# Split GELU multiply: outputs packed into the first load's buffer, 64 KB stores in place of separate output buffers

## Chip, cores, metric

One core of a Trainium2 chip. The metric is device time in microseconds; the granted clock was 1.00 in every run. Times are medians, with the range of the runs in brackets. A run over 1.5% above the fastest of its kernel counts as slow and is left out.

## The reference

```python
x: float32 [32, 512, 2048]
x1, x2 = x[..., :1024], x[..., 1024:]
return 0.5 * x1 * (1 + erf(x1 / sqrt(2))) * x2     # float32 [32, 512, 1024]
```

134.2 MB are read and 67.1 MB written. Per output element there is one GELU (ScalarE, "ACT" in the profile) and one multiply (VectorE, "DVE").

## The kernel before

The 16384 rows are cut into 16 tiles of 8 rows on each of 128 partitions. Loads go out from SyncE ("SP", queue q1), stores from ScalarE (queue q10). Two load buffers of 64 KB a partition and two output buffers of 32 KB take 192 KB.

```python
R, STEP = 8, 4
x_t = x_flat.rearrange("(n p r) d -> n p r d", p=P, r=R)
o_t = out_flat.rearrange("(n p r) d -> n p r d", p=P, r=R)
xpool = ctx.enter_context(tc.tile_pool(name="xpool", bufs=2))
opool = ctx.enter_context(tc.tile_pool(name="opool", bufs=2))
# ... cut: load(i) is one nc.sync.dma_start of a whole tile
ahead = [load(0), load(1)]
for i in range(n_tiles):
    x_tile = ahead.pop(0)
    o_tile = opool.tile([P, R, half], out.dtype, name="o_tile")
    for r in range(0, R, STEP):
        rows = slice(r, r + STEP)
        nc.scalar.activation(out=x_tile[:, rows, :half], in_=x_tile[:, rows, :half], func=GELU)
        nc.vector.tensor_mul(out=o_tile[:, rows, :], in0=x_tile[:, rows, :half], in1=x_tile[:, rows, half:])
        # ... cut: the last tile is stored in two halves
    # ... cut: the last two tiles are stored from nc.sync
    store(nc.scalar, i, o_tile, slice(0, R))
    if i + 2 < n_tiles:
        ahead.append(load(i + 2))
```

## Time and profile before

| | before |
|---|---|
| time | 471.43 us (471.22 to 471.63, 5 runs) |
| span of the profiled run | 469.7 us |
| ACT busy / DVE busy | 115.2 us / 140.2 us |
| DMA rate over the span / in mid-kernel | 429 / 434 GB/s |
| one tile: load in flight, store in flight | 45.5 us, 41.8 us (medians from issue to landing) |

Read it from the bottom up: a load and a store are in flight all the time, the rate does not move (434 GB/s in every stretch of 58 us from 57 to 405 us), and the compute engines wait for it (ACT 340.5 us for loads, DVE 321.6 us for ACT). (Issue is the moment at which an instruction starts a transfer, landing the moment at which its completion is signalled.)

### The profile page before, as it was taken

Reading aid. Unit: us, or ns where it says so; the run is one execution under the profiler, and the core shown is the slowest. Engines: PE = TensorE matmul, PEld = TensorE weight load, DVE = VectorE, ACT = ScalarE, POOL = GpSimd, SP = SyncE. Lnnn points to the kernel's source line nnn. Section 1 sums busy time; section 2 is a strip of 40 time slices with the busy share of each in tenths; the row PEclk is TensorE's granted clock in tenths of the full one; section 3 lists DMA queues with packets and bytes.
Section 4 is the critical chain, followed back from the end, with each engine's and each line's share of the span. In section 5 each row is a group of like instructions: output and inputs, shape, how many; then the busy total and the mean of one; then the engine's idle time right before and its main releaser. Section 6 shows DMA issues by size and latency. Waiting matters only on the chain.

```text
span 469.7 us, 213 instructions
## 1 busy us (share of the span) xinstructions
DVE 140.2 (30%) x32; ACT 115.2 (25%) x33; POOL 0.2 (0%) x4
## 2 busy tenths in 40 slices
DVE  0070704307042070520606115060250702507043
ACT  1052306023060320603206041060500505005060
POOL 0000000000000000000000000000000000000000
DMA  8999999999999999999999999999999999999988
GB/s 357 446 446 357 446 446 446 402 446 458 391 446 444 433 463 402 435 413 491 402 419 430 491 402 402 446 491 402 402 446 480 413 402 444 449 446 402 474 375 357
DMA packets 4754, 201.35 MB, mean 429 GB/s; under 512 B 528, under 2 KB 528, under 8 KB 528
## 3 DMA queue, kind: packets, MB, share of 16 engines
q1 hardware_dynamic: 2736, 142.61, 70.5%
q10 hardware_dynamic: 2016, 58.72, 29.0%
q14 instruction: 2, 0.02, 0.0%
HBM read 134.22 MB, written 67.11 MB: 429 GB/s over the span
## 4 chain that ended last, share of the span: by engine, by line
DMA 77%; DVE 14%; ACT 6%; DVEq 1%; issue 0%; SPq 0%; ACTq 0%
DMA x_tile<-in_x_dram 77%; DVE o_tile L57 14%; ACT x_tile L54 6%; DVEq L93 1%; SPq L41 0%; ACTq L54 0%
## 5 line engine op out<-in xcount | busy, mean ns | idle before, releaser
L57 DVE TENSOR_TENSOR o_tile<-x_tile 128x4096 f32<-128x4096 f32 x32 | 140.2, 4422 | 321.6 <-ACT x_tile L54 321.6
L54 ACT ACTIVATE x_tile<-x_tile 128x4096 f32<-128x4096 f32 x32 | 114.0, 3608 | 340.5 <-DMA x_tile<-in_x_dram 340.5
L54 ACT ACT_TABLE_LOAD x1 | 1.3, 1283 | 0.7 <-PEq L82 0.7
L82 POOL MEMSET const-bfloat16-1.0<- 128x1 bf16 x1 | 0.1, 102 | 0.0
L82 POOL MEMSET const-uint8-127<- 128x1 uint8 x1 | 0.1, 101 | 0.0
L82 POOL MEMSET const-float32-0.0<- 128x1 f32 x1 | 0.1, 99 | 0.2 <-issue 0.2
L82 POOL MEMSET const-float32-1.0<- 128x1 f32 x1 | 0.1, 98 | 0.0
## 6 DMA issues: line engine op xcount, KB each, us to landing
out_dram<-o_tile ACTq DMA_DIRECT2D x14, 4096.0 KB, 41.8
out_dram<-o_tile SPq DMA_DIRECT2D x1, 4096.0 KB, 24.8
out_dram<-o_tile SPq DMA_DIRECT2D x2, 2048.0 KB, 6.9
x_tile<-in_x_dram SPq DMA_DIRECT2D x16, 45.5
```

What stands on the lines that cost most here:

```text
L54: nc.scalar.activation(out=x_tile[:, rows, :half], in_=x_tile[:, rows, :half], func=GELU)
L57: nc.vector.tensor_mul(out=o_tile[:, rows, :], in0=x_tile[:, rows, :half], in1=x_tile[:, rows, half:],)
L82: nc = _bacc.Bacc("TRN2", target_bir_lowering=False, num_devices=1)
L93: with _tile.TileContext(nc) as tc:
```

## The change

Intent: a third full load buffer instead of output buffers, and stores as long as loads. A block is now 16 rows a partition, read as two loads A and B of 8 rows each. A has two buffers, B one. A's outputs overwrite A's first half, row by row behind the reading; B's outputs go into A's second half. The whole A buffer, 64 KB a partition, is then one store. The diff is shortened: "..." and the comments mark cuts, and the helpers `load`, `gelu` and `gelu_mul` are left out.

```diff
-    R, STEP = 8, 4
-    x_t = x_flat.rearrange("(n p r) d -> n p r d", p=P, r=R)
-    o_t = out_flat.rearrange("(n p r) d -> n p r d", p=P, r=R)
+    R = 8
+    x_t = x_flat.rearrange("(n p h r) d -> n h p r d", p=P, h=2, r=R)
+    o_t = out_flat.rearrange("(n p r) d -> n p r d", p=P, r=2 * R)
...
-    xpool = ctx.enter_context(tc.tile_pool(name="xpool", bufs=2))
-    opool = ctx.enter_context(tc.tile_pool(name="opool", bufs=2))
+    apool = ctx.enter_context(tc.tile_pool(name="apool", bufs=2))
+    bpool = ctx.enter_context(tc.tile_pool(name="bpool", bufs=1))
...
+    ahead = [load(0), load(1), load(2)]
+    for n in range(n_blocks):
+        a_tile, b_tile = ahead.pop(0), ahead.pop(0)
+        last = n == n_blocks - 1
+        gelu(a_tile, slice(0, 4))
+        gelu(a_tile, slice(4, R))
+        for lo, hi in ((0, 1), (1, 2), (2, 4), (4, 8)):
+            gelu_mul(slice(lo, hi), a_tile, a_tile[:, lo * half : hi * half])
...                                # last block: store A's half from nc.sync
+        for lo, hi in ((0, 4), (4, 8)):
+            gelu(b_tile, slice(lo, hi))
+            o = a_tile[:, (R + lo) * half : (R + hi) * half]
+            gelu_mul(slice(lo, hi), b_tile, o)
...                                # last block: store each quarter from nc.sync
+        if not last:
+            nc.scalar.dma_start(out=o_t[n], in_=a_tile.rearrange("p (r d) -> p r d", d=half))
+        for k in (2 * n + 3, 2 * n + 4):      # B of the next block, A of the one after
+            if k < 2 * n_blocks:
+                ahead.append(load(k))
```

Two waits are new. The next B load waits for the multiplies on the only B buffer. The A load after next waits for the landing of the whole store, since the store reads the buffer that this load fills; below it is called the **A reload**.

More of the change, by code (lines that the diff above doesn't have):

```diff
@@ L29 @@
     half = dim // 2
-    R, STEP = 8, 4
-    x_t = x_flat.rearrange("(n p r) d -> n p r d", p=P, r=R)
-    o_t = out_flat.rearrange("(n p r) d -> n p r d", p=P, r=R)
-    n_tiles = x_t.shape[0]
-    xpool = ctx.enter_context(tc.tile_pool(name="xpool", bufs=2))
-    opool = ctx.enter_context(tc.tile_pool(name="opool", bufs=2))
-    def load(i):
-        x_tile = xpool.tile([P, R, dim], x.dtype, name="x_tile")
-        nc.sync.dma_start(out=x_tile, in_=x_t[i])
-        return x_tile
-    def store(queue, i, o_tile, rows):
-        queue.dma_start(out=o_t[i][:, rows, :], in_=o_tile[:, rows, :])
@@ L47 @@
-    ahead = [load(0), load(1)]
-    for i in range(n_tiles):
-        x_tile = ahead.pop(0)
-        o_tile = opool.tile([P, R, half], out.dtype, name="o_tile")
-        last = i == n_tiles - 1
-        for r in range(0, R, STEP):
-            rows = slice(r, r + STEP)
-            nc.scalar.activation(
-                out=x_tile[:, rows, :half], in_=x_tile[:, rows, :half], func=GELU
-            )
-            nc.vector.tensor_mul(
-                out=o_tile[:, rows, :],
-                in0=x_tile[:, rows, :half],
-                in1=x_tile[:, rows, half:],
-            )
-            if last:
-                store(nc.sync, i, o_tile, rows)
-        if not last:
-            store(nc.sync if i == n_tiles - 2 else nc.scalar, i, o_tile, slice(0, R))
-        if i + 2 < n_tiles:
-            ahead.append(load(i + 2))
+    R = 8
@@ new lines, with load @@
+    x_t = x_flat.rearrange("(n p h r) d -> n h p r d", p=P, h=2, r=R)
+    o_t = out_flat.rearrange("(n p r) d -> n p r d", p=P, r=2 * R)
+    n_blocks = x_t.shape[0]
+    apool = ctx.enter_context(tc.tile_pool(name="apool", bufs=2))
+    bpool = ctx.enter_context(tc.tile_pool(name="bpool", bufs=1))
+    def load(n):
+        n, h = divmod(n, 2)
+        pool, name = (bpool, "b_tile") if h else (apool, "a_tile")
+        t = pool.tile([P, R * dim], x.dtype, name=name)
+        nc.sync.dma_start(out=t.rearrange("p (r d) -> p r d", d=dim), in_=x_t[n, h])
+        return t
@@ new lines, in gelu_mul, with gelu @@
+    def gelu_mul(rows, t, o):
+        i = t.rearrange("p (r d) -> p r d", d=dim)[:, rows, :]
+        nc.vector.tensor_mul(
+            out=o.rearrange("p (r d) -> p r d", d=half), in0=i[:, :, :half], in1=i[:, :, half:]
+        )
+    def gelu(t, rows):
+        i = t.rearrange("p (r d) -> p r d", d=dim)[:, rows, :half]
+        nc.scalar.activation(out=i, in_=i, func=GELU)
+    ahead = [load(0), load(1), load(2)]
[6 more added lines that the diff above has]
+            gelu_mul(slice(lo, hi), a_tile, a_tile[:, lo * half : hi * half])
+        if last:
+            nc.sync.dma_start(
+                out=o_t[n][:, :R, :],
+                in_=a_tile[:, : R * half].rearrange("p (r d) -> p r d", d=half),
+            )
+        for lo, hi in ((0, 4), (4, 8)):
+            gelu(b_tile, slice(lo, hi))
+            o = a_tile[:, (R + lo) * half : (R + hi) * half]
+            gelu_mul(slice(lo, hi), b_tile, o)
+            if last:
+                nc.sync.dma_start(
+                    out=o_t[n][:, R + lo : R + hi, :],
+                    in_=o.rearrange("p (r d) -> p r d", d=half),
+                )
+        if not last:
+            nc.scalar.dma_start(
+                out=o_t[n], in_=a_tile.rearrange("p (r d) -> p r d", d=half)
+            )
+        for k in (2 * n + 3, 2 * n + 4):
+            if k < 2 * n_blocks:
+                ahead.append(load(k))
```

## The prediction

Passages whose figures no trace of this case shows are cut from the text on record: one whole paragraph; in step 3 the times of the multiplies, which came to a sum of 144 us of DVE time, and the line that expects this sum; in the rivals the size of a loss by pitch and the arguments for and against it, and a limit of the rate; in step 4 a reason for the first store's wait. The sum of the forecast, its terms: 471.4 us, plus 0 or 6.5, plus 0 to 6, so 471.4 to 483.9, put at 473.5 within 470.0 to 479.5. The DVE time is not one of them.

> **What bounds the kernel now.** I read the page of the kernel before first, because its busy shares and its DMA slices say at once whether a compute engine or the transfers set the time.
>
> ```profile
> span 469.7 us, 213 instructions
> ...
> DVE 140.2 (30%) x32; ACT 115.2 (25%) x33; POOL 0.2 (0%) x4
> ...
> DMA  8999999999999999999999999999999999999988
> ...
> q1 hardware_dynamic: 2736, 142.61, 70.5%
> q10 hardware_dynamic: 2016, 58.72, 29.0%
> ...
> HBM read 134.22 MB, written 67.11 MB: 429 GB/s over the span
> DMA 77%; DVE 14%; ACT 6%; DVEq 1%; issue 0%; SPq 0%; ACTq 0%
> ```
>
> The compute engines are idle more than two thirds of the time. The DMA digit is 9 in every slice but the first and the last two, and the packets of the two queues took 70.5 + 29.0 = 99.5% of what 16 engines have in the span. The chain's "DVE 14%, ACT 6%" must not be read as 20% to be won: the chain follows a load back to the multiply that freed its buffer, but the DMA engines went on with other transfers during that multiply. The view by stretches of time settles it; its last two columns are DMA share and GB/s, the second from the left is the length:
>
> ```profile
> 57.00:115.00 58.00, 17.52 (x4) 14.25 (x4) 0.00 (x0) 1.00 1.00 434
> 173.00:231.00 58.00, 17.52 (x4) 14.24 (x4) 0.00 (x0) 1.00 1.00 434
> 440.00:470.00 30.00, 8.76 (x2) 7.12 (x2) 0.00 (x0) 1.00 0.90 385
> ```
>
> Two tiles in 58.0 us, again and again, with the DMA share at 1.00 and 434 GB/s. Two tiles are 16.78 MB in and 8.39 MB out, 25.17 MB / 434 GB/s = 58.0 us. So nothing but bytes is in the middle of the kernel, and all of 134.22 + 67.11 = 201.33 MB at 434 GB/s is 463.9 us. The other 5.8 us of the span are at the ends. From the timeline and the single packet records of the trace: the first load is issued at 0.73 us and its first packet moves at 1.7; the first packet of each engine takes 0.7 us longer than the 2.42 us of all later 64 KB packets; when the very first store joins the loads, at about 42 us, the load packet ahead of it takes 3.1 to 3.8 us instead of 2.42, 1.1 us more on the mean of the 16 engines; and the last bytes move at 468.2, 1.5 us before the end. That is 5.0 us; the rest is small gaps and the rounding of 434.
>
> Last, how the two queues share the engines, from the DMA view of the stretch 50 to 60 us (packets, MB, share):
>
> ```profile
> q1 hardware_dynamic: 48, 3.15, 72.5%
> q10 hardware_dynamic: 48, 1.57, 36.4%
> ```
>
> Equal counts of packets, twice the bytes: q1, all loads here, moves 64 KB a packet (8 rows of 8 KB), q10, all stores, 32 KB (8 rows of 4 KB). Loads and stores alternate packet by packet. That is why a 4 MB store that needs 9.7 us alone takes a median 41.8 us from issue to landing: at a third of the rate it needs 29.0 us, and it queues behind the store before it.
>
> [...]
>
> **The change, part by part.**
>
> 1. Bytes: none saved. A block of 16 rows a partition still reads 16.78 MB and writes 8.39 MB. Loads keep 64 KB packets, now from rows 128 KB apart; stores go from 32 KB to 64 KB packets, so 14 of them become 7. The gain of fewer packets is nil, as 32 KB packets already move at the full rate (1.00 share, 434 GB/s with both kinds).
>
> 2. SBUF: 2 x 64 + 2 x 32 = 192 KB a partition before, 2 x 64 + 64 = 192 KB after. The third full load buffer replaces the output buffers.
>
> 3. ACT: the same 32 GELUs, 115 us. DVE: per block 2 multiplies of 1024, one of 2048 and 3 of 4096 in place of 4 of 4096. [...] All of it lies beside transfers.
>
> 4. Waits. Before, each load needs only its own buffer's multiplies. Now the first load of a block (A) may be issued only when the whole store of two blocks ago has landed, because its buffer holds the outputs; the second (B) needs the multiplies on the single B buffer. Whether a queue runs dry is a matter of a cycle that I follow by hand, with 8.39 MB / 434 = 19.3 us for 8 MB alone, and 12.4 us from the landing of B to its last multiply (before: 22.67 to 35.11 us). A0 lands at 22.7, B0 at 42.0, A1's last byte would move at 60.5. B0 is computed at 54.5: store 0 and load B1 are issued. The first store of before was issued at 35.1 and moved its first packet at 42.3[...]. So store 0 and B1 both start at about 60.5, right as A1 ends. Now both have 64 KB packets, share half and half, and need 38.7 us: both end at about 97 to 99. If the store has the first turn it ends one packet (2.4 us) before B1 on each engine. Load A2 is issued at the landing (about 0.4 us after the last record) and can move 1.0 us later (from 457.45 to 458.3 us in the tail of before a new transfer took 0.9 us). So A2 arrives just as B1's last packet finishes. B1 lands at 100, A2 runs alone for the 12.4 us of B1's computing, has 6 us left when store 1 and B2 are issued at 112.5, and the cycle repeats, 58.0 us later. The margin is only about 1 us, but it corrects itself: if A2 is late by a little, the next store is ahead of it by as much.
>
> 5. The join. Before, stores are always two deep after the first, so a store joins a load-only stream once. After, the store queue empties in each block, so a store joins afresh 7 times. If each join costs the 1.1 us seen once, that is 6 x 1.1 = 6.5 us more. If that was a first-use cost, nothing.
>
> 6. Ends. Start: unchanged. Tail: A7's half store (4 MB) is queued behind B7 on the same queue, then two stores of 2 MB (4.8 us each) behind it: B7's last byte at about 448, then 457.7, 462.5, 467.3; the multiplies are ready at 452, 456.5 and 461, ahead of their turns. The same end as before, within 0.5 us.
>
> Sum: 471.4 us (the span plus 1.7), plus 0 or 6.5 us for the joins, plus 0 to 6 us for late A loads.
>
> **The rivals.** First, the new wait on the store bites: if B goes ahead of the store, A2 is issued about 1.4 us after the last packet of both, up to 2 us idle in each of 6 reloads, up to 12 us or 2.5%, to about 483. For it: the nearly equal ends in step 4. Against it: the self-correction, which lets it happen once or in part. Second, the 128 KB pitch costs rate[...]. Third, a gain: the chain shows DVE and ACT on 20% of the path, which a third load buffer seems to take out. That would be worth 90 us if it were real; the 1.00 DMA share speaks against it[...].
>
> **Range and chances.** About half of the weight lies on 470.5 to 472 (bytes only), a third on 475 to 479 (joins or late loads in each block), the rest above. Between these I put 473.5, with 470.0 to 479.5 as the range. 2% below, 462.0, is less than the bytes need at 434 GB/s, so faster has 1%. 2% above is 480.9, which needs two of the losses together: 9%.
>
> **What would show it.** The DMA share should stay near 1.00 with a repeat of 58.0 us a block; 59 us with dips at the joins would show step 5; a share under 0.98 just before each A load, with the load's issue waiting for the store, the first rival; a rate below 434 in stretches with share 1.00, the second. Stores should land about 43 us after issue, and in a stretch where both queues run they should now have equal bytes. [...] I am wrong if the span is below 467 or above 479.

## The result

484.27 us (483.16 to 485.49, 5 runs), slower: ratio 1.0267, 95% interval 1.0248 to 1.0286. A ratio here is the mean time of one kernel's fast runs over that of the other's of the same rounds, so not quite the ratio of the medians. The range of the prediction ended at 479.5. The changed kernel also scatters by 2.3 us, where the kernel before scatters by 0.4.

The page of the changed kernel, the lines that answer to those shown of before:

```profile
span 481.1 us, 204 instructions
...
DVE 143.4 (30%) x48; ACT 115.2 (24%) x33; POOL 0.2 (0%) x4
...
DMA  8999999999999999999999999999999999999988
...
q1 hardware_dynamic: 2736, 142.61, 70.7%
q10 hardware_dynamic: 1008, 58.72, 28.2%
...
HBM read 134.22 MB, written 67.11 MB: 419 GB/s over the span
...
DMA b_tile<-in_x_dram 58%; DMA out_dram<-a_tile 18%; DVE a_tile L50 10%; DMA a_tile<-in_x_dram 6%; ACT b_tile L56 5%; DVEq L114 1%; SPq L44 0%; ACTq L56 0%
```

The digits of the DMA row are the same 9s as before, and still 11 us are gone: a tenth is too coarse, and a packet that takes longer than most still counts as busy (below, a share of 0.99 at 417 GB/s). The rate over the span says it (419 instead of 429 GB/s), and the chain has a new member: a store, 18% of the path, where before no store was on it. The same line of the kernel before, then the transfers of both kernels, first before, then changed (number, size where given, median us from issue to landing):

```profile
DMA x_tile<-in_x_dram 77%; DVE o_tile L57 14%; ACT x_tile L54 6%; DVEq L93 1%; SPq L41 0%; ACTq L54 0%
...
out_dram<-o_tile ACTq DMA_DIRECT2D x14, 4096.0 KB, 41.8
x_tile<-in_x_dram SPq DMA_DIRECT2D x16, 45.5
```

```profile
b_tile<-in_x_dram SPq DMA_DIRECT2D x8, 47.1
out_dram<-a_tile ACTq DMA_DIRECT2D x7, 43.9
```

The stretches of time from one block's store to the next, and then the end. From the left: the stretch, its length, DVE, ACT, POOL, granted clock, DMA share, GB/s.

```profile
54.35:113.53 59.18, 17.93 (x6) 14.24 (x4) 0.00 (x0) 1.00 1.00 425
113.53:172.22 58.69, 17.93 (x6) 14.25 (x4) 0.00 (x0) 1.00 1.00 427
172.22:232.78 60.56, 17.93 (x6) 14.25 (x4) 0.00 (x0) 1.00 0.99 417
232.78:293.08 60.30, 17.93 (x6) 14.24 (x4) 0.00 (x0) 1.00 0.99 417
293.08:352.61 59.53, 17.93 (x6) 14.24 (x4) 0.00 (x0) 1.00 1.00 424
352.61:412.25 59.64, 17.93 (x6) 14.24 (x4) 0.00 (x0) 1.00 1.00 419
412.25:481.00 68.75, 17.93 (x6) 14.24 (x4) 0.00 (x0) 1.00 0.94 399
```

A block needs 58.0 us of bytes. Each takes 0.7 to 2.6 us more, with the share near 1.00 and the rate down to 417. The loss is spread over the kernel, a little in each block. (The views count a packet where it starts, so the rate of a short stretch is coarse: 33 us of the changed kernel without any loss, 62 to 95, show 413 GB/s. Sizes of losses below are from packet records.)

What the queue of SyncE, which issues all loads, waits for (total us, times, longest):

```profile
SPq L44 <- DMA out_dram<-a_tile: 260.2, 6, 44.2
SPq L44 <- DVE a_tile L50: 87.2, 7, 12.5
```

The first line is the new wait: all six A reloads stand behind the landing of a store, for up to 44.2 us each. The wait alone does not say what it costs: e13, below, has six of them too (156.6 us in all), and its reloads lost 0.01 us or less. So the question is what other loads the DMA engines have left by then.

To see this I went below the views, to the trace's records of single packets. A load or store of 8 MB is 8 packets of 64 KB on each of 16 engines (2944 packets for the 16 loads and the 7 stores of the changed kernel). 88% of them took 2.418 us within 10 ns, in the kernel before 97%, and that is 434 GB/s on 16 engines. The records do not name the engine, but each packet starts within some ns of another's end, which chains them to 16 sequences of 208 packets. The loss in a stretch is then the time between packets plus what packets take beyond 2.418 us, over 16 engines. Over the whole span this gives 16.5 us in the changed kernel and 4.8 in the one before, a difference of 11.7 against 11.4 of span. A store joins when its first packets go out on engines that only loads were using. The next store is issued 15 to 17 us after an A reload and joins 3 to 8 us later. Around each reload and each such join the records give (us lost, mean of 16 engines):

| A reload issued at | lost at the reload | lost when the next store joins |
|---|---|---|
| 96.2 | 0.00 | 0.03 |
| 157.2 | 0.59 | 1.56 |
| 216.9 | 0.68 | 1.38 |
| 277.0 | 0.48 | 1.16 |
| 336.7 | 0.39 | 1.19 |
| 397.1 | 1.56 | 0.74 |
| sum | 3.7 | 6.1 |

The rest is 0.5 us in the middle of the second block and 1.4 us at the end. There A's half store was through before the first of B's two quarter stores had been issued (468.89 us), seen in the DMA share of these stretches of the changed kernel:

```profile
460.00:465.00 5.00, 0.57 (x1) 4.21 (x2) 0.00 (x0) 1.00 0.97 419
465.00:470.00 5.00, 5.00 (x2) 2.91 (x1) 0.00 (x0) 1.00 0.67 288
```

The table already asks the question of the experiments. The store joins a load-only stream seven times; is it the join that costs, or is it the reload before it, which in this trace was on time just once, the once that the join was free (the first store of the kernel, which no reload precedes, aside)?

### The profile page after: what moved, and what is told of

It reads as the page before. It is cut to its first block, busy times and chain, and to the rows that moved or that the text cites. A ratio compares the mean times of both kernels' runs of the same rounds, so it can differ in the third digit from the quotient of the medians.

```text
span 481.1 us, 204 instructions
## 1 busy us (share of the span) xinstructions
DVE 143.4 (30%) x48; ACT 115.2 (24%) x33; POOL 0.2 (0%) x4
## 3 DMA queue, kind: packets, MB, share of 16 engines
q10 hardware_dynamic: 1008, 58.72, 28.2%
## 4 chain that ended last, share of the span: by engine, by line
DMA 82%; DVE 10%; ACT 5%; DVEq 1%; issue 0%; SPq 0%; ACTq 0%
DMA b_tile<-in_x_dram 58%; DMA out_dram<-a_tile 18%; DVE a_tile L50 10%; DMA a_tile<-in_x_dram 6%; ACT b_tile L56 5%; DVEq L114 1%; SPq L44 0%; ACTq L56 0%
## 5 line engine op out<-in xcount | busy, mean ns | idle before, releaser
L50 DVE TENSOR_TENSOR a_tile<-b_tile 128x4096 f32<-128x4096 f32 x16 | 70.1, 4422 | 182.3 <-ACT b_tile L56 182.3
L50 DVE TENSOR_TENSOR a_tile<-a_tile 128x1024 f32<-128x1024 f32 (+2 forms) x32 | 73.3, 2292 | 147.5 <-ACT a_tile L56 146.1
L56 ACT ACTIVATE b_tile<-b_tile 128x4096 f32<-128x4096 f32 x16 | 57.0, 3608 | 200.0 <-DMA b_tile<-in_x_dram 200.0
L56 ACT ACTIVATE a_tile<-a_tile 128x4096 f32<-128x4096 f32 x16 | 57.0, 3608 | 151.9 <-DMA a_tile<-in_x_dram 151.9
## 6 DMA issues: line engine op xcount, KB each, us to landing
out_dram<-a_tile ACTq DMA_DIRECT2D x7, 43.9
```

What stands on the lines that cost most here:

```text
L50: nc.vector.tensor_mul(out=o.rearrange("p (r d) -> p r d", d=half), in0=i[:, :, :half], in1=i[:, :, half:])
L56: nc.scalar.activation(out=i, in_=i, func=GELU)
```

## The experiments

The rounds ran on three chips. Each time stands beside runs of the kernel before in the same rounds, whose medians were 471.39 to 471.69 us.

| run | what differs | us (range, 4 runs) | ratio to before |
|---|---|---|---|
| e1 | changed, stores on the loads' queue | 473.03 (472.56 to 473.42) | 1.0029 |
| e2 | changed, B loaded in two halves | 480.67 (480.25 to 482.58) | 1.0202 |
| e3 | before, loads in two halves | 476.37 (475.25 to 478.84) | 1.0110 |
| e4 | before, rows 128 KB apart | 471.62 (471.31 to 471.73) | 1.0001 |
| e5 | changed, A's half stored early | 471.88 (471.61 to 472.01) | 1.0007 |
| e7 | changed, store 1.2 us earlier | 479.40 (475.56 to 480.84) | 1.0155 |
| e8 | changed, store 0.8 us later | 488.58 (486.48 to 489.82, 3 fast runs) | 1.0353 |
| a0 | changed, again | 484.96 (483.39 to 485.77) | 1.0281 |
| e11 | changed, store in 12 and 4 rows | 495.60 (495.09 to 496.08) | 1.0515 |
| e12 | changed, B computed in one piece | 528.38 (527.44 to 529.90) | 1.1211 |
| e13 | changed, B load held back | 473.07 (472.30 to 473.63) | 1.0023 |
| e6 | changed, store in two pieces of 32 KB | 471.77 (471.51 to 472.04) | 0.9996 |

The first theory was that of the prediction's step 5, plus late reloads: each join costs 1.1 us, late reloads some 3 us.

### e1: the store on the queue of the loads

```diff
-            nc.scalar.dma_start(
+            nc.sync.dma_start(
                 out=o_t[n], in_=a_tile.rearrange("p (r d) -> p r d", d=half)
```

> The changed kernel with its block stores issued from SyncE, on the queue of the loads, ahead of the B load. A store then never joins from an empty second queue, it runs before B, and A's reload is issued some 19 us ahead of its turn. Theory (joins cost about 1.1 us each and late A reloads some 3 us, both because two queues share half and half): 470 to 472 us, DMA share 1.00 in the middle, no stretch of lower rate. Rival 1 (waits on the single B buffer or on in-place outputs cost the time): stays at 482 to 485. Rival 2 (rows read 128 KB apart are slower): stays at 482 to 485.

473.03 us, 1 us above the range but with 11 of the 13 us back. In-place outputs, the single B buffer, the smaller multiplies and the 128 KB rows are all still there, so none of them is the loss. The 1.5 us above the kernel before lie at the end (1.8 us by the packet records, at 460 to 464 us). The block stretches of e1 show it:

```profile
113.65:171.95 58.30, 17.93 (x6) 14.24 (x4) 0.00 (x0) 1.00 1.00 432
171.95:230.29 58.34, 17.93 (x6) 14.25 (x4) 0.00 (x0) 1.00 1.00 431
```

One thing did not fit: the very first store still cost 1.1 us in the packet records, though it is on the loads' own queue, and the later ones 0.02 to 0.2. So it is with the first store in all 14 traces (0.8 to 1.3 us by the packet records; 1.1 in the kernel before, 1.0 in the changed one), on either queue. The 1.1 us that I had seen in the kernel before came with the first store of a kernel, and says nothing of joins.

### e4: the layout in memory alone

```diff
-    x_t = x_flat.rearrange("(n p r) d -> n p r d", p=P, r=R)
+    x_b = x_flat.rearrange("(n p h r) d -> n h p r d", p=P, h=2, r=R)   # o_b likewise
+    x_t = [x_b[i // 2, i % 2] for i in range(n_tiles)]
```

> The kernel before with the changed kernel's layout in memory: 64 KB a partition read from rows 128 KB apart, 32 KB stores 64 KB apart; all else as before. Theory (queues alone): 471 to 472 us. [...]

471.62 against 471.55 us: rows 128 KB apart cost nothing here. The second rival of the prediction, the pitch, is out.

### e3: joins without a load that waits for a store

```diff
-        nc.sync.dma_start(out=x_tile, in_=x_t[i])
+        for r in range(0, R, STEP):
+            nc.sync.dma_start(out=x_tile[:, r : r + STEP, :], in_=x_t[i][:, r : r + STEP, :])
```

> The kernel before, with each load cut into two of 32 KB a partition, the size of a store's packets. Loads and stores then share half and half, a 4 MB store is done in about 19 of each 29 us, its queue runs empty, and each of some 14 stores joins afresh; output buffers, waits and bytes stay. Theory (about 1.1 us a join): 471.4 + 13 x 1.1 = 486 us, within 482 to 488. Rival (joins are free after the first, only the late reload of the changed kernel costs): 471 to 472.

476.37 us, between the two. The trace decides: the store queue does run empty and the stores join afresh, but after the first there is no loss at any join. The stretches of e3 in mid-kernel are near the full rate; what it lost is at its end.

```profile
206.94:317.80 110.86, 30.98 (x7) 28.06 (x8) 0.00 (x0) 1.00 1.00 433
440.00:474.00 34.00, 9.66 (x3) 7.23 (x2) 0.00 (x0) 1.00 0.85 363
```

So a join in itself is free here, and step 5 of the prediction falls. (The end: by then the 16 engines were 4 us apart, and the last store ended with the slowest.)

### e2: the reload made early by B's packet size

```diff
-        nc.sync.dma_start(out=t.rearrange("p (r d) -> p r d", d=dim), in_=x_t[n, h])
+        t3 = t.rearrange("p (r d) -> p r d", d=dim)
+        for lo, hi in ((0, 4), (4, 8)) if h else ((0, 8),):
+            nc.sync.dma_start(out=t3[:, lo:hi, :], in_=x_t[n, h][:, lo:hi, :])
```

> The changed kernel with the B load cut into two of 32 KB a partition, so that the store (64 KB packets, other queue) takes two thirds while they share and lands some 9 us before B's second half. A's reload is no longer late, but a store still joins from an empty queue in each block. Theory (joins 6.4 us, late reloads about 3 us, tail about 1.4): 479 to 482 us. Rival (the late A reload is the whole loss): 471 to 473. Rival (neither): 484.

480.67 us, inside the range of the first theory, and for the wrong reason. The reload was early, as meant, and up to 348 us neither reloads nor joins lost more than 0.2 us each, although the store joined from an empty queue each time. The loss came late:

```profile
229.91:347.80 117.89, 36.04 (x12) 28.71 (x8) 0.00 (x0) 1.00 1.01 434
405.00:450.00 45.00, 10.85 (x5) 8.49 (x3) 0.00 (x0) 1.00 0.97 380
450.00:479.00 29.00, 8.85 (x2) 5.87 (x2) 0.00 (x0) 1.00 0.82 348
```

The time alone would have confirmed the join theory. What happens between 405 and 450 is taken up at e12.

### e5: the half of A stored as soon as it is ready

```diff
-        if last:
-            nc.sync.dma_start(
+        if True:
+            (nc.sync if last else nc.scalar).dma_start(
                 out=o_t[n][:, :R, :],
...
-                out=o_t[n], in_=a_tile.rearrange("p (r d) -> p r d", d=half)
+                out=o_t[n][:, R:, :],
+                in_=a_tile[:, R * half :].rearrange("p (r d) -> p r d", d=half),
```

> The changed kernel with each block's store cut into two of 4 MB on ScalarE's queue: the half of A as soon as A is computed, the half of B at the block's end. Packets are 32 KB again, the store queue is always one deep, and the last half of a block lands some 9 us before B's load ends, so the A reload is early. Theory (the loss comes from the single late 8 MB store, on which the A reload hangs): 471 to 474 us. Rival (in-place outputs or one B buffer cost in themselves): 482 to 485.

471.88 us: level with the kernel before, without output buffers and with in-place outputs. Its order of stores is that of the kernel before again, so it tests the late store and the joins together, not each alone.

### e7, e8, a0: the store a little earlier or later

Here I had a second theory: that the issue of the store falls just on a packet's end, so that the 16 engines decide differently and run out of step. (In the trace of the changed kernel six engines moved their first packet of the second store at 117.0 to 117.3 us, the other ten at 119.4 to 120.2; that a packet's end made the difference was my theory.)

```diff
-        for lo, hi in ((0, 4), (4, 8)):
+        for lo, hi in ((0, 4), (4, 8)) if last else ((0, 2), (2, 5), (5, 8)):    # e7
+        for lo, hi in ((0, 4), (4, 8)) if last else ((0, 5), (5, 8)):            # e8
```

> The changed kernel with B's GELU and multiply in three pieces of 2, 3 and 3 rows instead of two of 4: the store and the next B load are issued about 1.1 us earlier after B has landed, half a 64 KB packet (2.42 us). In the changed kernel the time from B's last packet to the moment its store can be taken up is just about 6 packets, so the 16 engines, 0.5 us apart, decide differently at the second join and are 2.9 us apart from then on, where before they stay within 0.6. New theory (falling out of step is what costs: landings wait for the slowest engine, reloads come late for the fast ones): the join is mid-packet for all engines, spread stays under 1 us, 471 to 474 us. Rival (each join of a store costs 1.1 us by itself): 478 to 481. Rival (the reload's tie alone): 480 to 485.

> The changed kernel with B's GELU and multiply in pieces of 5 and 3 rows: store and B load are issued about 0.9 us later. New theory: the join is again away from a packet's end, so engines agree and the spread stays small, but the store takes its turn one packet later than in e7, so the A reload has only about half a microsecond to spare: 472 to 479 us. Rival (joins cost each): 478 to 481. Rival (every microsecond later is a loss): 486 to 492.

> The changed kernel once more, on the same chip as e5, e7 and e8, for its time there and for a second trace of where the engines fall out of step. All theories: 483 to 485.5 us; new theory: the spread of a landing over the 16 engines grows from 0.5 to over 2 us within the first three blocks again.

e7 took 479.4, e8 488.6, the unchanged a0 484.96 us. The second theory fell: e8 was to be about as good as e7 and was the worst, and in e7 the engines still came to be over 4 us apart. What the three show is a slope: by the timelines the store went out 1.2 us earlier in e7 and 0.8 us later in e8, and that gave 5.6 us and cost 3.6, some 4.6 us for each us. That is not far from the six reloads of a kernel times the shift. It points to a loop without slack, from B's landing over its multiplies and the store to the A reload. This is the third theory: a late reload costs, and a join costs only after one. The packet records agree. In the trace of e7 two of six reloads lost nothing, and the joins after them lost 0.04 us or less; after its other four they lost 0.7 to 1.4. In e8 and a0 all twelve reloads lost something, and every join after them lost 0.9 to 1.6.

The records also show what "late" means. Take the time from the issue of a reload to the moment when the first engine runs out of B packets. Of the 30 reloads of the changed kernel, a0, e7, e8 and e13 (below), the 9 with 2.9 us or more lost nothing and their joins were free, though in three of them (one of the changed kernel, two of e7) the next store and B load were issued together, as they are after the late ones. The 21 with 2.5 us or less lost 0.07 to 2.0 us, and their joins 0.7 to 1.6.

### e11: the store in two unequal pieces

```diff
+        if not last:                    # both of B's GELUs first
+            gelu(b_tile, slice(0, 4))
+            gelu(b_tile, slice(4, 8))
...
-        if not last:
-            nc.scalar.dma_start(out=o_t[n], in_=a_tile.rearrange("p (r d) -> p r d", d=half))
+            else:                       # after B's first and second multiply
+                f = 0 if lo == 0 else R + lo
+                nc.scalar.dma_start(
+                    out=o_t[n][:, f : R + hi, :],
+                    in_=a_tile[:, f * half : (R + hi) * half].rearrange("p (r d) -> p r d", d=half))
```

> The changed kernel with a block's store in two, both on ScalarE's queue after B's GELUs: 12 of 16 rows as soon as B's first multiply is done (4.4 us earlier than now), the last 4 rows where the whole store is issued now. The queue of stores still runs empty in each block, so a store joins afresh 7 times, but it has landed some 3 to 5 us before B's load ends and the A reload is no longer late. Third theory (what costs is the A reload arriving late, and the joins cost only after a late reload): 471 to 475 us. Rival (each join costs 1.1 us by itself): 477 to 481. Rival (only bytes and order matter, not this wait): 484.

495.6 us, 20 above what I expected, and the mistake is instructive. In these traces the engines took turns by packets, not bytes: 48 of 64 KB and 48 of 32 KB from 50 to 60 us of the kernel before. Two pieces are 16 packets an engine, 8 of 48 KB and 8 of 16 KB (q10 has 2016 records in e11, 1008 in the changed kernel), and some 10 load packets are left to take turns with. So the small last piece, issued at the same moment as the whole store before, lands 51.1 us after its issue where the whole store took 43.9:

```profile
out_dram<-a_tile ACTq DMA_DIRECT2D x7, 6144.0 KB, 38.5
out_dram<-a_tile ACTq DMA_DIRECT2D x7, 2048.0 KB, 51.1
```

Instead of making the reload early I had made it fully late. The DMA share now shows it at the first reload, and the rate at the join after it (e11, stretches as above):

```profile
98.00:104.00 6.00, 1.08 (x1) 4.73 (x2) 0.00 (x0) 1.00 0.85 322
107.00:115.00 8.00, 4.67 (x2) 0.00 (x0) 0.00 (x0) 1.00 0.99 360
```

By the packet records the engines stood idle for 1.8 to 2.5 us at each reload, and the join after it lost 1.05 to 1.34 us, six times out of six. And here the 16 engines ended a store within 0.4 to 1.2 us of each other, in three of the six blocks within 0.5, so being out of step is not what makes the join dear.

### e12: the store 3.4 us later

```diff
-        for lo, hi in ((0, 4), (4, 8)):
+        for lo, hi in ((0, 4), (4, 8)) if last else ((0, 8),):
```

> The changed kernel with B's GELU and multiply in one piece of 8 rows: the store and the next B load are issued 3.4 us later after B's landing than in the changed kernel (7.1 + 8.7 = 15.8 us instead of 12.4). e7 and e8 gave about 5 us of time for each us of that delay. Third theory (the loop from B's landing over store, landing and A reload is closed, each us of delay is paid about 5 times): 484.5 + 3.4 x 5 = 501 us, within 495 to 506. Rival (a packet boundary is being hit or missed): no steady slope, 478 to 492. Rival (transfers hide the compute): unchanged, 483 to 486.

528.38 us: later is dearer, but 27 us beyond the line drawn through e7 and e8. The packet records show something more. In this trace, after A's last packet, an engine turned first either to the store or to the B load. In four of the seven blocks of e12 most of the engines (13 to 16) turned to B first; while the two then shared, the engines lost 5.4 to 5.9 us on the mean, 3.7 to 4.3 of it on B's packets and 1.5 to 1.7 on the store's. In the three blocks in which all engines turned to the store first they lost less than 0.1. Where B went first it was also done before the store, and the reloads after three of these blocks lost 5.2 to 6.1 us; the others lost 0.7 to 1.5. Two stretches of e12, first B first, then store first (its 415 is the full rate, as coarse as the 413 above):

```profile
62.00:105.00 43.00, 9.16 (x4) 6.48 (x2) 0.00 (x0) 1.00 0.94 352
134.00:167.00 33.00, 9.17 (x4) 7.12 (x2) 0.00 (x0) 1.00 0.96 415
```

The same happened in e2, to 2 engines in its sixth block (5.4 us each, the other 14 lost 0.2) and to 11 in its last (5.6 us each, the others 2.1): that is the stretch from 405 to 450. In the changed kernel, in a0, e7, e8 and e13 no engine did so. Why the order of the first turn should matter was not found.

### e13: a load held back

```diff
-    def load(n):
+    def load(n, after=None):
...
+        if after is not None:
+            nc.vector.tensor_copy(out=t[:, :1], in_=after[:, half : half + 1])
         nc.sync.dma_start(out=t.rearrange("p (r d) -> p r d", d=dim), in_=x_t[n, h])
...
-                ahead.append(load(k))
+                ahead.append(load(k, ahead[0] if k % 2 else None))
```

> The changed kernel with only the B load held back: it is issued not beside the store but when the next A has landed, some 7 us later (a one-column copy from that A tile into the B tile makes it wait). The store then has the engines to itself for one or two packets and ends one or two packets further ahead of B, so the A reload is issued in time, by delaying a load and nothing else; the store still joins from an empty queue 7 times. Third theory (a late A reload costs, and a join costs only after one): 471.5 to 475 us, no stretched packets at the joins after the first. Rival (each join costs 1.1 us by itself): 477 to 481. Rival (holding a load back in a transfer-bound kernel costs what it is held back): 490 to 530.

473.07 us. This is the plainest test: nothing was taken away, one load was issued later, and 11 of the 13 us came back. The store is through earlier against B, so the reload is on time:

```profile
114.52:172.58 58.06, 18.08 (x7) 14.25 (x4) 0.00 (x0) 1.00 1.01 436
172.58:230.60 58.02, 18.08 (x7) 14.24 (x4) 0.00 (x0) 1.00 1.01 437
```

These are 58.0 us a block, where the changed kernel has 58.7 and 60.6 us. Store queue and joins are as in the changed kernel; all six reloads and the six joins after them lost 0.01 us or less. And the engines are 4 to 5 us apart in this trace, which cost nothing until the end (1.7 us, at 456 to 464 us).

### e6: smaller store packets

```diff
-            nc.scalar.dma_start(out=o_t[n], in_=a_tile.rearrange("p (r d) -> p r d", d=half))
+            for lo, hi in ((0, R), (R, 2 * R)):
+                nc.scalar.dma_start(
+                    out=o_t[n][:, lo:hi, :],
+                    in_=a_tile[:, lo * half : hi * half].rearrange("p (r d) -> p r d", d=half))
```

> The changed kernel with a block's store cut into two of 32 KB a partition, both issued where the whole one is. A store now has 16 packets an engine, taking turns with only about 10 load packets, so it ends some 7 us after B's load and every A reload finds the queue of loads dry. Third theory (an exposed reload about 2.6 us of the engines, as e11's trace shows, and the join after it 1.2 us, 6 times): 471.4 + 6 x 3.8 = 494 us, within 489 to 500. Rival (smaller store packets are as good as in the kernel before, which has them): 471 to 485.

471.77 us, which looks like a refutation and is a failed experiment. The timeline of e6 shows the first half's store issued right behind A's multiplies, long before B's GELUs:

```profile
77.20 9.34 DVE L50 TENSOR_TENSOR a_tile<-a_tile 128x1024 f32<-128x1024 f32 x4 [20.32 <-ACT a_tile L56]
86.58 0.34 ACTq L84 DMA_DIRECT2D out_dram<-a_tile  x1
98.83 0.33 SPq L44 DMA_DIRECT2D a_tile<-in_x_dram  x1
102.51 7.12 ACT L56 ACTIVATE b_tile<-b_tile 128x4096 f32<-128x4096 f32 x2 [21.83 <-DMA b_tile<-in_x_dram]
```

The first half depends on A alone, so it was moved up ahead of them (86.58 against 102.51 us), and e6 became e5 over again. It confirms e5 and says nothing of what it was made for. The issue order should have been read before the run.

## Why the prediction was wrong

**Right.** What bounds the kernel: no undisturbed stretch was faster than the 434 GB/s of the kernel before by more than the coarseness of the view (437 in a block of e13), no version was faster than the kernel before beyond noise, and the third rival (a gain) never appeared. DVE busy 143.4 us against 140.2, beside transfers as step 3 said (1.23, 2.29 and 4.42 us for a multiply of 1024, 2048 and 4096, measured here), ACT unchanged at 115.2, no cost of pitch (e4), half and half sharing by equal packets (5.24 MB on each queue from 65 to 90 us of the changed kernel), stores landing in 43.9 us (43 predicted). The places of the loss were named, too: the A reload, and the joining of the store.

**The failed step is step 4**, the hand-followed cycle. It found that the A reload arrives just as B's last packet finishes, called the margin about 1 us, and let it pass with the words that it corrects itself. It did not: the cost rose with the delay of the store, 479.4 us with the store 1.2 us earlier (e7), 484.3 as changed, 488.6 with 0.8 us later (e8), 528.4 with 3.4 us later (e12). I read it so: a store that is issued later also lands later, B with it, and the loop closes over B's landing. The trace shows five of six reloads late, by 0.4 to 1.6 us of engine time each, 3.7 us in all.

The terms of that margin were mis-sized (us, from the packet records of the changed kernel):

| term | step 4 | measured |
|---|---|---|
| end of the store's last data to end of B's last data | 2.4 | 4.8 or 7.2 on one engine; slowest engine's store to first engine's B: 6.7 in the first block, 3.3 to 4.2 in the five late ones |
| end of the store's last data to the reload's issue | 0.4 | 2.8, six of six |
| reload's issue to its first packet on an idle engine | 1.0 | 0.95 to 1.0 (e11) |
| left over | 1.0 | 2.9 in the first block (on time), -0.5 to 0.4 in the late ones |

Two things were missed. The trace has a record of 4 bytes for each engine on the store's queue (112 for the 7 stores), and the reload is issued 0.35 to 0.40 us after the last of a store's 16, six of six. Beside loads this record starts 2.41 us after the data, the time of one 64 KB packet, which I read as the wait for a turn. The kernel before shows the same 2.41 us at all 14 stores on ScalarE's queue. Where no load was left to take turns with, the reload was issued 0.4 to 0.5 us after the data (e11), as step 4 had it. And with the last of 16 records the landing waited for the slowest engine; step 4 took the 16 as one. In the first block they ended a store 0.5 us apart, after it 2.0 to 3.1 us, which used up the rest of a lead that was longer than predicted.

**Step 5 had the right size by luck, and the wrong cause.** The sum for the joins, 6.5 us or nothing, against 6.1 measured in the profiled run, looks like a hit. But the 1.1 us it was taken from belongs to the first store of a kernel (it is there in e1, on a single queue, and the later joins are nearly free), joins of a well fed stream were free (0.2 us or less in e2 up to 348 us, 0.01 or less in e13, no loss after the first in e3), and in every trace of the changed kernel's form a join cost 0.7 to 1.6 us exactly when the reload before it had lost time. So the two losses that the prediction added as separate chances are one: where the reload was late, both were paid. That is why a sum that put half of its weight on neither was wrong; with both, its own figures reach 483.9, which is near the measured 484.27 but rests on that borrowed 1.1 us.

**Step 6** took the end as unchanged within 0.5 us; it cost 1.4 us, since B landed too late for its quarter stores to follow without a gap.

**What stays open.** Why a join after a late reload stretched the last load packets ahead of it by about 1.2 us, whether the engines were in step (e11) or not (a0); why a reload issued 2.5 us ahead already lost time, when one moved 0.95 to 1.0 us after its issue (e11); and why an engine that turned to the B load before the store lost some 5.5 us while the two shared (e12, e2). All three are regular in the packet records, and none is explained. That the late reload is the root is shown by e13, which delays one load and removes both losses; e5 agrees, but removes the joins too.

No version beat the kernel before. e5 and e6 are level with it (ratios 1.0007 and 0.9996), as the bytes at 434 GB/s let expect.

## What to carry to other kernels

When a buffer's reload hangs on a store, follow the loop from landing over compute and store back to the load in packets and turns. Here the store's completion took a turn of its own (2.41 us), the slowest of the 16 engines set the landing (2.0 to 3.1 us behind the first), and a lead of 2.5 us or less, about a packet, lost time at 21 of 21 reloads. Where the margin is thin, what helped here was to store what is ready early (e5, 471.88 us), to put the store ahead of the next load on one queue (e1, 473.03), or to hold the competing load back (e13, 473.07). In this transfer-bound kernel the order of transfers cost 13 us with the same bytes, and a DMA share of 0.99 hid it (417 GB/s instead of 434): divide bytes by time for each period of the loop. An experiment whose time agrees with a theory may do so for another reason (e2), and one that disagrees may not be the experiment you meant (e6): read its trace before either is used.
